# The first w_up gate columns of a decoder layer: low weights of the second unit taken by both token tiles at once, and a unit's high products set between the transposes of the second tile

## The chip, the cores and the metric

The kernel runs on one core of a Trainium2 chip. The metric is the device time of one execution in microseconds (us). The profile names the engines PE (matrix products), PEld (its weight loads), ACT, DVE, POOL and SP; SP issues most transfers.

## The reference

One decoder layer on 256 tokens of 2048 features, float32 throughout. The first half of the layer mixes tokens (two kinds of attention and an output projection), and adds the normalised result to the residual x. The change lies where the second half begins:

```python
x = x + rmsnorm(mix, post_mix_g[l])
h = rmsnorm(x, pre_ffn_g[l])
u = causal_dwconv(h @ w_up[l], conv_w[l], conv_b[l])      # w_up: 2048 x 11264
gate, val = jnp.split(u, 2, axis=-1)
y = (jax.nn.gelu(gate, approximate=True) * val) @ w_down[l]
x = x + rmsnorm(y, post_ffn_g[l])
```

## The kernel before

**Products.** Every float32 number is split in two: a high part that PE takes as it is (`whi` for weights, the first half of `hT` for the activations) and a low part, the number less its high part (`wlo`, the second half of `hT`). A product is high by high, high by low and low by high, added up in one PSUM bank. The activations stand transposed in `hT`, 16 blocks of 128 features; a block's 512 columns are the high parts of 256 tokens and then the low parts. So a block of high weights takes all 512 columns in one matmul, and a block of low weights takes 256.

**Weights.** `w_up` comes in units of 512 features by 256 columns: SP loads a unit into one of five `raw` buffers (L113), ACT makes `whi` by a copy that rounds (L168; L151 for the units named below), and DVE makes `wlo` by a subtraction that reads `raw` and `whi` (L171; L154). The `raw` buffer can be loaded again after the subtraction. Four units make the 2048 features of 256 columns.

**The first gate columns.** `first_gate` computes the first 256 gate columns, in two banks, while x and its transposes are still being made for one token tile after the other. Its four units were loaded and rounded earlier (`gate_unit`). `turn(t, n)` puts four 128x128 transposes of tile t on PE (L819), and returns two functions that fill `hT` from them: `high` on ACT (L824) and `low` on DVE (L829). Tile 1's transposes need x of tile 1, which DVE makes in four steps of 512 features (`residual`, L812). `one(t, u)` multiplies unit u for tile t: eight high matmuls over that tile's 128 high and 128 low columns (L1002), then low matmuls (L998). For units 2 and 3 (`both`) the low matmuls are left out for tile 0, and take all 256 tokens when tile 1 has come; for units 0 and 1 each tile has its own, of 128 tokens.

**After it.** `proj_T4` multiplies the first 256 value columns, then the second group of 256 gate columns, then its values, and so on. It takes four units: high products of the first and second unit (L340), their low products (L346), then low products of the third and fourth, and their high products. When a group's banks are full, each of its two blocks goes through the convolution: ACT copies half of the bank (L960), DVE adds the other half (L962), POOL multiplies by the row of norms (L963), ACT scales (L967), DVE adds two more taps (L973, L975). ACT then applies the gelu to gates (L1231), and DVE multiplies gates by values (L1249) and makes sums for the next product (L1029 to L1038, with G split by L368 and L369).

**What sets the order.** PE's order is that of the code. Around `first_gate` the same holds for ACT, DVE and POOL among their own instructions there (`order`, left right after `first_gate`). For what follows, the roundings and the convolution, a scheduler that builds the program sets each engine's order, and it may put the later roundings between the earlier work. Each engine then takes its instructions in that fixed order, and waits at the first one that isn't ready.

Of the kernel before, what the change touches and what calls it, by code (L numbers as in the profile page):

```python
# [34 lines left out]
def hybrid_layer(ctx: ExitStack, tc: tile.TileContext, x, pre_mix_g, w_in, b_forget, sinks,  # L35
# [16 lines left out]
    def bank(tag="acc"):  # L52
        return ps.tile([P, 512], F32, tag=tag, bufs=4, name="bank_" + tag)
# [9 lines left out]
    def later(n, f):  # L63
        todo.setdefault(now[0] + n, []).append(f)
# [306 lines left out]
    with tc.tile_pool(name="mixp", bufs=1) as mp:  # L371
# [442 lines left out]
        def turn(t, n):  # L814

            tb = bank("att")
            for j in range(4):
                c = n * 512 + j * P
                pe.transpose(tb[:, j * P:(j + 1) * P], x_sb[:, t, c:c + P], ident)  # L819
            kts = [(n * 4 + j, tb[:, j * P:(j + 1) * P]) for j in range(4)]  # L820

            def high():
                for kt, b in kts:
                    act.activation(hT[:, kt, t * P:(t + 1) * P], b, AF.Copy,  # L824
                                   scale=gcol[:, 16 + kt:17 + kt])

            def low():
                for kt, b in kts:
                    dve.scalar_tensor_tensor(hT[:, kt, 256 + t * P:256 + (t + 1) * P], b,  # L829
                                             gcol[:, 16 + kt:17 + kt],  # L830
                                             hT[:, kt, t * P:(t + 1) * P].bitcast(F32),
                                             op0=ALU.mult, op1=ALU.subtract)

            return high, low

        def x_squares(t):
            for n in range(4):
                act.activation(junk, x_sb[:, t, n * 512:(n + 1) * 512], AF.Square,
                               accum_out=sq2[t][:, n:n + 1])
# [63 lines left out]
    with tc.tile_pool(name="ffn", bufs=1) as fp:  # L903
# [7 lines left out]
        def ffn_tables():  # L911
            for t in range(2):
                st2 = small.tile([P, 1], F32, tag="st", name="st_x")
                dve.tensor_reduce(st2, sq2[t], axis=AX.X, op=ALU.add)
                dffn.append(diag_of(rstd_of(st2, D, f"rffn{t}")))

            def rows():
                cbk = bank("att")
                for k in range(4):
                    pe.transpose(cbk[:, k * 88:(k + 1) * 88], cst[:, k, :], ident[:88, :88])  # L920
                dve.tensor_copy(cw.rearrange("p k c -> p (k c)"), cbk[:, :352])
                dve.tensor_copy(rowf, row_of(dffn, bank("att")))

            return rows
# [54 lines left out]
        def first_gate():  # L979

            banks = [bank(), bank()]

            def one(t, u):
                ts = slice(t * P, t * P + P)

                both = u >= 2
                ls = slice(0, 256) if both else ts

                def v(x):
                    return x.rearrange("p (h t c) -> p h t c", h=2, t=2)[:, :, t, :]  # L990

                for low in (False, True)[:1 if both and t == 0 else 2]:
                    for kt in range(u * 4, u * 4 + 4):
                        hi, lo = gate[kt]
                        for m, b in enumerate(banks):
                            ms = slice(m * P, (m + 1) * P)
                            if low:
                                pe.matmul(b[:, 256 + ls.start:256 + ls.stop], lo[:, ms],  # L998
                                          hT[:, kt, ls], start=False,
                                          stop=(t == 1 and kt == KT - 1))  # L1000
                            else:
                                pe.matmul(v(b), hi[:, ms], v(hT[:, kt, :]),  # L1002
                                          start=(t == 0 and kt == 0), stop=False)

            one(0, 0)
            one(0, 1)
            one(0, 2)
            for high, low in [turn(1, u) for u in range(4)]:
                high()
                low()  # L1010
            one(0, 3)
            lows[2]()
            x_squares(0)
            x_squares(1)
            for t in range(2):
                act.dma_start(x_dram[t * P:(t + 1) * P, :], x_sb[:, t, :])
            rows = ffn_tables()
            for u in range(4):
                one(1, u)
            later(1, rows)  # L1020
            return banks
# [189 lines left out]
        for half in range(2):  # L1211
# [5 lines left out]
            for g in range(FHALF // 2):  # L1217
                c0 = (half * (FHALF // 2) + g) * 256
                alt = g % 2
                if half == 0 and g == 0:  # L1220
                    bg = first_gate()
                    order.__exit__(None, None, None)
                    bv = [bank(), bank()]
                    proj_T4(w_up, DFF + c0, bv)
                else:
                    bg = [bank("att"), bank("att")] if alt else [bank(), bank()]
                    proj_T4(w_up, c0, bg)
# [174 lines left out]
```

## Time and profile before

| what | value |
|---|---|
| median of 3 runs | 1056.29 us (1055.24 to 1056.49) |
| the profiled execution's own time | 1056.47 us |
| its span, first to last instruction | 1054.7 us |
| PE busy | 1040.4 us (99%) |
| DVE busy | 840.8 us (80%) |
| ACT busy | 660.5 us (63%) |
| POOL busy | 268.0 us (25%) |
| the first gate columns on PE | 334.49 to 349.29 us |
| the first value columns | 349.29 to 361.11 us |
| the second gate columns | from 361.11 us |

A row of the timeline has the start in us from the span's start, the time from there to the end of the last instruction merged into it, engine, line, operation, out<-in, shapes, the count, and in brackets the idle time before it with what ended it. Matmuls overlap: a row's start less the start of the row before it is what PE needs for that row. A row of another engine can overlap the next one a little in the same way.

### The profile page before, as it was taken

The page shows a single profiled execution, that of the slowest core. Times are in us where ns is not written, and L with a number is a line of the kernel's source. Part 1 is how long each engine was busy: PE and PEld are TensorE (multiplying, and loading weights), DVE is VectorE, ACT ScalarE, POOL GpSimd, SP SyncE. Part 2 cuts the span into 40 slices and gives each one's busy share as a digit, 9 for nine tenths or more (in the row PEclk, how much of TensorE's full clock was granted, in tenths as well). Part 3 has the DMA queues.
Part 4 walks back from the last instruction along what each step waited for, and adds up shares of the span by engine and source line. Part 5 has one row for each costly group of instructions (what it writes and reads, how often), then busy time and mean ns, then how long its engine had stood idle before and what let it go on. Part 6 is the DMA issues. An engine that isn't in the chain of part 4 may idle for free.

```text
span 1054.7 us, 16573 instructions
## 1 busy us (share of the span) xinstructions
PE 1040.4 (99%) x5854; PEld 907.1 (86%) x5854; DVE 840.8 (80%) x1371; ACT 660.5 (63%) x1126; POOL 268.0 (25%) x312
## 2 busy tenths in 40 slices
PE   9999999999999999999999999999999999999996
PEld 7889988888889988888888888888888888888885
DVE  5988887787467888778877799867788788779996
ACT  6767666676655865566656675646555666567771
POOL 3254325442022224232232000013223223210004
PEclk9999999999999999999999999999999999999998
DMA  8978999988872899899999796899999999969893
GB/s 282 318 240 289 296 300 304 358 251 299 318 260 68 263 250 270 222 253 258 230 244 265 262 406 192 288 237 222 284 229 243 244 233 265 232 223 384 293 410 131
DMA packets 177470, 279.98 MB, mean 265 GB/s; under 512 B 9052, under 2 KB 133244, under 8 KB 176124
## 3 DMA queue, kind: packets, MB, share of 16 engines
q1 hardware_dynamic: 162432, 249.51, 69.3%
q0 software_dynamic: 13952, 26.74, 17.8%
q10 hardware_dynamic: 1004, 2.68, 0.6%
q8 instruction: 46, 0.75, 0.3%
q14 instruction: 36, 0.29, 0.1%
HBM read 274.55 MB, written 57.69 MB: 315 GB/s over the span
## 4 chain that ended last, share of the span: by engine, by line
PE 93%; DVE 2%; DMA 2%; POOL 1%; ACT 1%; issue 1%; SPq 0%; DVEq 0%; POOLq 0%; ACTq 0%
PE bank_acc L340 16%; PE bank_att L340 14%; PE bank_acc L365 12%; PE bank_att L1044 12%; PE bank_acc L346 8%; PE bank_acc L1044 7%; PE bank_att L346 7%; PE bank_acc L309 7%; PE bank_acc L314 4%; PE bank_att L531 1%; PE bank_att L566 1%; DMA gbc_ffn<-in_post_ffn_g_dram 1%; DVE wlo L171 1%; PE bank_acc L1002 1%; POOL y_sb L1307 1%
## 5 line engine op out<-in xcount | busy, mean ns | idle before, releaser
L171 DVE TENSOR_TENSOR wlo<-raw,whi 128x1024 fp32r<-128x1024 f32 (+3 forms) x271 | 334.2, 1245 | 94.6 <-ACT whi L168 86.9
L168 ACT CAST whi<-raw 128x1024 fp32r<-128x1024 f32 (+3 forms) x270 | 273.7, 1029 | 103.5 <-issue 45.0
L963 POOL TENSOR_TENSOR room<-room,rowf 128x256 f32<-128x256 f32 x88 | 95.8, 1109 | 331.6 <-DVE room L962 329.8
L340 PE MATMUL bank_acc<-hT,whi 128*128 128x512 f32 x736 | 173.3, 390 | 0.0
L340 PEld LDWEIGHTS bank_acc<-hT,whi 128*128 128x128 f32 x736 | 136.4, 188 | 27.4
L340 PE MATMUL bank_att<-hT,whi 128*128 128x512 f32 x640 | 150.6, 390 | 0.0
L340 PEld LDWEIGHTS bank_att<-hT,whi 128*128 128x128 f32 x640 | 118.7, 188 | 23.9
L967 ACT ACTIVATE room<-room,cw 128x256 f32<-128x256 f32 x88 | 52.5, 601 | 65.3 <-POOL room L963 65.0
L346 PEld LDWEIGHTS bank_acc<-hT,wlo 128*128 128x128 f32 x736 | 89.3, 188 | 2.0
L346 PE MATMUL bank_acc<-hT,wlo 128*128 128x256 f32 x736 | 89.8, 279 | 0.0
L309 PE MATMUL bank_acc<-hT,whi 128*128 128x512 f32 x352 | 88.0, 395 | 0.0
L1044 PE MATMUL bank_att<-whi,G 128*128 128x512 f32 x258 | 87.9, 389 | 0.0
L365 PE MATMUL bank_acc<-whi,oT 128*128 128x512 f32 (+1 forms) x272 | 81.8, 379 | 0.0
L369 DVE TENSOR_TENSOR wlo<-raw,whi 128x1024 fp32r<-128x1024 f32 (+1 forms) x66 | 71.4, 1102 | 10.3 <-ACT whi L368 9.6
L346 PEld LDWEIGHTS bank_att<-hT,wlo 128*128 128x128 f32 x640 | 77.6, 188 | 1.7
L346 PE MATMUL bank_att<-hT,wlo 128*128 128x256 f32 x640 | 77.9, 279 | 0.0
L973 DVE SCALAR_TENSOR_TENSOR room<-room,cw 128x256 f32<-128x256 f32 x88 | 59.2, 676 | 22.9 <-ACT room L967 22.9
L368 ACT CAST whi<-raw 128x1024 fp32r<-128x1024 f32 (+1 forms) x66 | 61.7, 953 | 23.2 <-issue 5.7
L309 PEld LDWEIGHTS bank_acc<-hT,whi 128*128 128x128 f32 x352 | 63.3, 188 | 11.6
L365 PEld LDWEIGHTS bank_acc<-whi,oT 128*128 128x128 f32 x272 | 50.2, 188 | 9.3
L1044 PEld LDWEIGHTS bank_att<-whi,G 128*128 128x128 f32 x258 | 48.4, 188 | 10.1
L365 PE MATMUL bank_acc<-wlo,oT 128*128 128x512 f32 (+1 forms) x136 | 51.2, 377 | 0.0
(269 smaller groups left out, 1757.3 us busy)
## 6 DMA issues: line engine op xcount, KB each, us to landing
raw<-in_w_up_dram SPq DMA_DIRECT2D x176, 512.0 KB, 5.6
raw<-in_w_in_dram SPq DMA_DIRECT2D x51, 512.0 KB, 6.4
raw<-in_w_down_dram SPq DMA_DIRECT2D x45, 512.0 KB, 6.9
raw<-in_w_out_dram SPq DMA_DIRECT2D x32, 512.0 KB, 7.0
t<-in_w_down_dram POOLq DMA_DIRECT2D x28, 512.0 KB, 9.2
raw<-t SPq DMA_DIRECT2D x26, 512.0 KB, 6.6
t<-t POOLq DMA_DIRECT2D x18, 512.0 KB, 8.6
extra<-t SPq DMA_DIRECT2D x14, 512.0 KB, 6.7
```

The source lines that it names most:

```text
L168: i1 = act.copy(hi[:, cs], raw[:, cs])
L171: i2 = dve.tensor_tensor(lo[:, cs], raw[:, cs], hi[:, cs].bitcast(F32), op=ALU.subtract)
L309: pe.matmul(b, parts[u][0][:, a, m * P:(m + 1) * P], hT[:, kt, :], start=(kt == 0), stop=(kt == KT - 1))
L340: pe.matmul(b, parts[u][0][:, a, m * P:(m + 1) * P], hT[:, kt, :], start=(kt == 0), stop=(kt == KT - 1))
L346: pe.matmul(b[:, 256:512], parts[u][1][:, a, m * P:(m + 1) * P], hT[:, kt, 0:256], start=False, stop=False)
L365: pe.matmul(b, a, r[:, cols], start=(first and i == 0), stop=(last and i == 2))
L368: act.copy(hi, src)
L369: dve.tensor_tensor(lo, src, hi.bitcast(F32), op=ALU.subtract)
L963: pool.tensor_tensor(u[:, 2:258], u[:, 2:258], rowf, op=ALU.mult)
L967: act.activation(y, u[:, 2:258], AF.Identity, bias=cw[:, 3, ch:ch + 1], scale=cw[:, 2, ch:ch + 1])
L973: dve.scalar_tensor_tensor(y, u[:, 1:257], cw[:, 1, ch:ch + 1], y, op0=ALU.mult, op1=ALU.add)
L1044: pe.matmul(b[:, to] if to else b, a, r[:, cols], start=(first and i == 0), stop=(last and i == 2))
```

## The change

For unit 1 too, the low weights now wait for both token tiles: `both` begins at unit 1. And `one(0, 3)`, which then consists of eight high matmuls, stands after the second `turn` of tile 1 and not after the fourth.

```diff
-                both = u >= 2
+                both = u >= 1
...
             one(0, 0)
             one(0, 1)
             one(0, 2)
-            for high, low in [turn(1, u) for u in range(4)]:
+            turned = []
+            for u in range(4):
+                turned.append(turn(1, u))
+                if u == 1:
+                    one(0, 3)
+            for high, low in turned:
                 high()
                 low()
-            one(0, 3)
             lows[2]()
```

PE around `first_gate` before, from `one(0, 0)` on (x8 is eight matmuls in a row, 128x2x128 the high product of one tile, L819 the transposes):

```order
L1002 MATMUL bank_acc<-hT_3701,whi 128x2x128 x8
L998 MATMUL bank_acc<-hT_3701,wlo 128x128 x8
L1002 MATMUL bank_acc<-hT_3701,whi 128x2x128 x8
L998 MATMUL bank_acc<-hT_3701,wlo 128x128 x8
L1002 MATMUL bank_acc<-hT_3701,whi 128x2x128 x8
L819 MATMUL bank_att<-ident,x_sb 128x128 x16
L1002 MATMUL bank_acc<-hT_3701,whi 128x2x128 x16
L998 MATMUL bank_acc<-hT_3701,wlo 128x128 x8
L1002 MATMUL bank_acc<-hT_3701,whi 128x2x128 x8
L998 MATMUL bank_acc<-hT_3701,wlo 128x128 x8
```

And now:

```order
L1002 MATMUL bank_acc<-hT_3701,whi 128x2x128 x8
L998 MATMUL bank_acc<-hT_3701,wlo 128x128 x8
L1002 MATMUL bank_acc<-hT_3701,whi 128x2x128 x16
L819 MATMUL bank_att<-ident,x_sb 128x128 x8
L1002 MATMUL bank_acc<-hT_3701,whi 128x2x128 x8
L819 MATMUL bank_att<-ident,x_sb 128x128 x8
L1002 MATMUL bank_acc<-hT_3701,whi 128x2x128 x8
L998 MATMUL bank_acc<-hT_3701,wlo 128x128 x8
L1002 MATMUL bank_acc<-hT_3701,whi 128x2x128 x8
L998 MATMUL bank_acc<-hT_3701,wlo 128x256 x8
```

Two groups of eight low matmuls of 128 tokens are gone, one of eight of 256 tokens has come, and the transposes stand in two lots with eight high matmuls between them.

The scheduler's order behind `first_gate` is another one as well. The second gate columns have four units, called A, B, C and D here: `whi_4371`, `whi_4378`, `whi_4416`, `whi_4423` before, and `whi_4363`, `whi_4370`, `whi_4408`, `whi_4415` now (the low part has the next number; the numbers of the two programs have nothing to do with each other). ACT before, where the first gate columns go through the convolution (`bank_acc_4034` is their second bank, `bank_acc_4227` and `bank_acc_4228` those of the first values; unit A's rounding stands five rows further up):

```order
L967 ACTIVATE room_4007<-room_4002,cw_4000 128x256
L960 COPY room_4002<-bank_acc_4034 128x256
L168 CAST whi_4378<-raw_4375 128x1024
L168 CAST whi_4416<-raw_4414 128x1024
L1231 ACT_TABLE_LOAD
L1231 ACTIVATE room_4007<-room_4007 128x256
L967 ACTIVATE room_4007<-room_4002,cw_4000 128x256
L960 COPY room_4002<-bank_acc_4227 128x256
L960 COPY room_4002<-bank_acc_4228 128x256
L168 CAST whi_4423<-raw_4420 128x1024
```

And now (the first values' banks are `bank_acc_4219` and `bank_acc_4220`):

```order
L967 ACTIVATE room_4007<-room_4002,cw_4000 128x256 x2
L168 CAST whi_4363<-raw_4361 128x1024
L1235 ACT_TABLE_LOAD
L1235 ACTIVATE room_4007<-room_4007 128x256 x2
L960 COPY room_4002<-bank_acc_4219 128x256
L960 COPY room_4002<-bank_acc_4220 128x256
L168 CAST whi_4370<-raw_4367 128x1024
L967 ACTIVATE room_4007<-room_4002,cw_4000 128x256 x2
L168 CAST whi_4408<-raw_4406 128x1024
L168 CAST whi_4415<-raw_4412 128x1024
```

Before, units A, B and C were rounded ahead of the copies of the first values' banks; now A alone is, and B, C and D stand behind them. (The change adds four lines, so L1231, L1249 and L1029 are L1235, L1253 and L1033 in the changed file.)

DVE before, at the same place; unit A's low part, `wlo_4372`, stands seven rows further up:

```order
L973 SCALAR_TENSOR_TENSOR room_4007<-room_4002,cw_4000,room_4007 128x256
L962 TENSOR_TENSOR room_4002<-bank_acc_4034,room_4002 128x256
L975 SCALAR_TENSOR_TENSOR room_4007<-room_4002,cw_4000,room_4007 128x256
L171 TENSOR_TENSOR wlo_4379<-raw_4375,whi_4378 128x1024
L171 TENSOR_TENSOR wlo_4417<-raw_4414,whi_4416 128x1024
L973 SCALAR_TENSOR_TENSOR room_4007<-room_4002,cw_4000,room_4007 128x256
L962 TENSOR_TENSOR room_4002<-bank_acc_4227,room_4002 128x256
```

And now:

```order
L171 TENSOR_TENSOR wlo_4364<-raw_4361,whi_4363 128x1024
L962 TENSOR_TENSOR room_4002<-bank_acc_4219,room_4002 128x256
L962 TENSOR_TENSOR room_4002<-bank_acc_4220,room_4002 128x256
L171 TENSOR_TENSOR wlo_4371<-raw_4367,whi_4370 128x1024
L973 SCALAR_TENSOR_TENSOR room_4007<-room_4002,cw_4000,room_4007 128x256 x2
L975 SCALAR_TENSOR_TENSOR room_4007<-room_4002,cw_4000,room_4007 128x256 x2
L1253 TENSOR_TENSOR room_4007<-room_4007 128x256 x2
L1033 TENSOR_TENSOR s_4348<-room_4007 128x128
L171 TENSOR_TENSOR wlo_4409<-raw_4406,whi_4408 128x1024
L369 TENSOR_TENSOR G1_4012<-room_4007,G1_4012 128x256
L1034 TENSOR_TENSOR room_4007<-room_4007 128x128
L171 TENSOR_TENSOR wlo_4416<-raw_4412,whi_4415 128x1024
```

The low parts of C and D stand behind the whole convolution of the first values now; C's stood ahead of it before. On SP and POOL no instruction has moved, and from the values of the second group on ACT and DVE have the same order as before, but for a few neighbours that have changed places.

## The prediction

> **What bounds the kernel now.** I read the page first, its busy times and its chain, and then the waits of PE over the whole span.
>
> ```profile
> PE 1040.4 (99%) x5854; PEld 907.1 (86%) x5854; DVE 840.8 (80%) x1371; ACT 660.5 (63%) x1126; POOL 268.0 (25%) x312
> PE 93%; DVE 2%; DMA 2%; POOL 1%; ACT 1%; issue 1%; SPq 0%; DVEq 0%; POOLq 0%; ACTq 0%
> ```
>
> ```profile
> PE bank_acc L390 <- DMA x_in<-in_x_dram: 1.3, 1, 1.3
> PE bank_acc L225 <- DVE junk L220: 1.3, 1, 1.3
> PE bank_att L590 <- DVE pl L369: 1.0, 1, 1.0
> PE bank_att L578 <- DVE pl L369: 0.5, 1, 0.5
> ```
>
> PE is busy 99% of the span and is 93% of the chain. The four waits are all that the list of PE's waits has, and their lines belong to the start and to attention. So behind attention PE runs without a pause, and two things follow: PE work that goes away is gained in full, and any new wait of PE is lost in full, since no later wait could take it up. The third view is the timeline of PE at the change.
>
> ```profile
> 335.44 1.00 PE L998 MATMUL bank_acc<-hT,wlo 128*128 128x128 f32 x8
> 336.28 1.16 PE L1002 MATMUL bank_acc<-hT,whi 128*128 128x256 f32 x8
> ...
> 339.12 1.91 PE L819 MATMUL bank_att<-ident,x_sb 128*128 128x128 f32 x16
> 340.79 2.16 PE L1002 MATMUL bank_acc<-hT,whi 128*128 128x256 f32 x16
> ...
> 346.46 1.10 PE L998 MATMUL bank_acc<-hT,wlo 128*128 128x256 f32 x8
> 347.40 1.12 PE L1002 MATMUL bank_acc<-hT,whi 128*128 128x256 f32 x8
> ...
> 349.29 3.81 PE L340 MATMUL bank_acc<-hT,whi 128*128 128x512 f32 x16
> 361.11 3.80 PE L340 MATMUL bank_att<-hT,whi 128*128 128x512 f32 x16
> 364.75 3.90 PE L346 MATMUL bank_att<-hT,wlo 128*128 128x256 f32 x32
> 368.48 3.82 PE L340 MATMUL bank_att<-hT,whi 128*128 128x512 f32 x16
> ```
>
> **Part one, the low products.** Eight low matmuls of 128 tokens take 336.28 - 335.44 = 0.84, eight of 256 tokens 347.40 - 346.46 = 0.94. Two of the first go and one of the second comes: 0.94 - 2 x 0.84 = -0.74. The weights for it are there long before.
>
> **Part two, the transposes.** One low group fewer stands ahead of them, so PE comes to them 0.84 earlier, at 338.28 instead of 339.12. What they need is x of tile 1:
>
> ```profile
> 337.35 2.74 DVE L812 SCALAR_TENSOR_TENSOR x_sb<-mix_sb,rmix,x_sb 128x512 f32<-128x512 f32 x4 [0.66 <-POOL rmix L239]
> 339.76 4.25 ACT L824 ACTIVATE hT<-bank_att,gcol 128x128 fp32r<-128x128 f32 x16 [3.81 <-PE bank_att L819]
> ```
>
> The four steps of DVE end about 338.1, 338.75, 339.4 and 340.1 (2.74 in four). The first four transposes (0.42, a quarter of 340.79 - 339.12) find theirs ready at 338.28; the second four, due at 338.70, wait for 338.75 and the signal's way, some 0.17. The eight high matmuls of unit 3 then take 1.0 of PE, and the last two lots start at 340.3, behind the fourth step. So the wait is 0.17, within 0 and 0.3; without the high matmuls between, the fourth lot would have been due at 339.6 and waited half a microsecond, and that cover is what the move buys. ACT begins its 16 copies at 338.9 and not 339.76, DVE its 16 low parts at 340.15, right behind the fourth step. Tile 1's first high matmul is due at 341.15 and finds its blocks just made, as before. The first gate columns then end at 349.29 - 0.74 + 0.17 = 348.72, a gain of 0.57. The squares and the diagonal for the row of norms come earlier too: ACT has one rounding (unit A's) fewer among them.
>
> **Part three, the roundings behind it.** This is where I expect the loss. The rows of before for the second gate columns: B and C on ACT, the copies ahead of D, D; on DVE A, then B and C, then D:
>
> ```profile
> 357.74 2.00 ACT L168 CAST whi<-raw 128x1024 fp32r<-128x1024 f32 x2
> 361.86 0.63 ACT L960 COPY room<-bank_acc 128x256 f32<-128x256 f32 x2
> 362.38 1.05 ACT L168 CAST whi<-raw 128x1024 fp32r<-128x1024 f32 x1
> 351.78 1.23 DVE L171 TENSOR_TENSOR wlo<-raw,whi 128x1024 fp32r<-128x1024 f32 x1
> 358.82 2.82 DVE L171 TENSOR_TENSOR wlo<-raw,whi 128x1024 fp32r<-128x1024 f32 x2
> 363.47 1.32 DVE L171 TENSOR_TENSOR wlo<-raw,whi 128x1024 fp32r<-128x1024 f32 x1
> ```
>
> PE wanted A's and B's high parts from 361.11, their low parts from 364.75, C's low part from 364.75 + 3.73/2 = 366.61 and D's 0.93 later. C's was ready at 361.6 and D's at 364.8: 5.0 and 2.7 in hand. Now B, C and D stand behind the copies L960 of the first values' banks, which can't start until PE has ended those values, at 361.11 - 0.57 = 360.54. From there:
>
> ACT copies two banks (0.52 to the next start: 362.38 - 361.86) and rounds B from 361.06 to 362.11. PE's eight high matmuls of A end at 360.54 + 3.64/2 = 362.36, so B comes in time, by a quarter of a microsecond.
>
> Behind the copies DVE adds both banks (360.95 to 361.70), and POOL multiplies (from 361.44 and 362.03). DVE could take B's low part at 362.17. How long this takes together is the unknown, and these rows bound it:
>
> ```profile
> 356.30 0.64 POOL L963 TENSOR_TENSOR room<-room,rowf 128x256 f32<-128x256 f32 x1 [1.84 <-DVE rowf L922]
> 358.51 0.91 POOL L963 TENSOR_TENSOR room<-room,rowf 128x256 f32<-128x256 f32 x1 [1.57 <-DVE room L962]
> 374.91 2.31 POOL L963 TENSOR_TENSOR room<-room,rowf 128x256 f32<-128x256 f32 x2 [7.77 <-DVE room L962]
> 374.41 0.75 DVE L962 TENSOR_TENSOR room<-bank_att,room 128x256 f32<-128x256 f32 x2
> 375.07 1.55 DVE L171 TENSOR_TENSOR wlo<-raw,whi 128x1024 fp32r<-128x1024 f32 x1
> ```
>
> Alone, the product L963 takes 0.64. At 358.51 it began 0.31 ahead of a subtraction, took 0.91, and the pair of subtractions took 2.82: with 1.2 for the second, 1.6 for the first. At 374.91 the subtraction began inside the first product and ahead of the second, which was held up: the two took 2.31, so the second 1.7. Whichever is first is nearly undisturbed. Here POOL's second product, at 362.03, is ahead of B's subtraction by 0.14: POOL ends at 362.7, and DVE is free again at 363.75. I take this, the nearest row being 358.51.
>
> The Trainium skill has a rule for it, on the page "SBUF — State Buffer", section "SBUF: two separate sides": DVE, when it reads two inputs in SBUF, and GpSimd share one pair of ports as an exclusive lock, and the one that starts second is blocked for the other's whole instruction. The trace agrees (0.64 alone, 1.7 behind a subtraction). By the rule the order of the two decides, and the sum is 1.5 or that of the first rival below; if they merely shared the speed, either order would cost alike, and that rival would go.
>
> Then ACT scales (L967, one after each product, to 363.3) and rounds C from 363.24 to 364.29. But DVE has the convolution of the values ahead of C's low part: two L973, two L975, two L1249, one L1029. Its length stands in these rows:
>
> ```profile
> 366.05 0.48 DVE L973 SCALAR_TENSOR_TENSOR room<-room,cw 128x256 f32<-128x256 f32 x1 [0.39 <-ACT room L967]
> ...
> 368.12 1.22 DVE L171 TENSOR_TENSOR wlo<-raw,whi 128x1024 fp32r<-128x1024 f32 x1
> 369.26 0.42 DVE L369 TENSOR_TENSOR G<-room,G 128x256 fp32r<-128x256 f32 x1
> ...
> 369.80 1.22 DVE L171 TENSOR_TENSOR wlo<-raw,whi 128x1024 fp32r<-128x1024 f32 x1
> ```
>
> 368.12 - 366.05 = 2.07 with one L973, and 0.4 more for the other: from 363.75 to 366.2. C's low part is made until 367.4 (1.22). PE, without a pause so far, wants it at 360.54 + 3.64 + 3.73/2 = 366.05, and waits till 367.45: **1.4**. Eight low matmuls of C later (0.93) PE wants D's, at 368.38. DVE first splits G and takes a difference (369.80 - 369.26 = 0.54) and then makes it, 367.3 + 0.54 + 1.22 = 369.05: a second wait, **0.7**. D's high part and those of the next units are there by then. After that DVE and ACT have PE's whole high products of C and D (3.65) to catch up in, and the order is the old one.
>
> The `raw` buffers come free later too: A's at 360.2, where it was 353.0 (351.78 and 1.2), C's at 367.4, where it was 361.6. The loads that SP issues into them are for the next values, and start 7 us later behind A, 3 to 6 behind the others:
>
> ```profile
> raw<-in_w_up_dram SPq DMA_DIRECT2D x176, 512.0 KB, 5.6
> 378.49 1.05 ACT L168 CAST whi<-raw 128x1024 fp32r<-128x1024 f32 x1 [4.70 <-DMA raw<-in_w_up_dram]
> ```
>
> Before, ACT waited 4.7 for such a load and PE did not notice. With 5.6 from issue to landing the load behind A lands at 366, and ACT wants it at 366.5; the one behind C lands at 373, and PE wants that unit's low part near 380. I cost this at nothing; at 10 us a load the cover would be just used up.
>
> **The sum**: -0.74 + 0.17 + 1.4 + 0.7 = +1.5. The profiled execution took 1056.47, its span 1054.7; the sum is a difference inside the span, so it would give 1058.0 for that execution. The median is 0.18 lower: **1057.8 us**. A measurement of this kernel tells about 0.2%, 2.1 us, from no change, so I forecast no change that can be told, on the slow side.
>
> **The rivals.**
>
> *The subtraction goes first.* If B's subtraction starts ahead of POOL's second product (0.14 decides), that one ends 0.6 behind it, as at 374.91: at 364.3 rather than 362.7. ACT scales till 364.95, rounds C till 365.9, DVE's convolution ends at 367.05, C's low part is there at 368.3 and D's at 370: waits of 2.3 and 0.7, and the sum is +2.45, **1058.75**, slower by 0.23%. For it speaks that the pair at 374.91 went this way; against it, that there the subtraction didn't have to wait for ACT, and here it does.
>
> *No wait.* If ACT and DVE keep ahead of PE in spite of their order (the copies of the banks could start earlier than I think, and C's low part come by 366), only the first two parts are left: -0.57, **1055.7**. For it speaks the 5.0 that C had in hand, and that ACT is busy 63% only; against it, that both engines take their rows in order, and that 1.4 has to be found in a chain whose links all have a row.
>
> *The loads are late.* If the loads behind C and D land 10 us after C's release and then wait in turn, the second group's values wait 1 to 2 us more: 1059.5. ACT's 4.7 at 378 speak for it, PE's lack of a wait there against.
>
> **How the numbers follow.** My case 0.62, the subtraction first 0.2, no wait or a small one 0.12, late loads 0.06. My case alone has 1057.1 to 1058.5, from the wait of part two (0 to 0.3) and 0.3 either way in each later wait. The range reaches from a small wait to the subtraction first: 1056.4 to 1059.1. Slower by over 0.2% (above 1058.4) are the second case, most of the last, and little of mine: 0.26. Faster by over 0.2% would need a gain of 2.1, where 0.74 is all that PE loses in work: 0.02. Within: 0.72.
>
> **What would show it.** In the profile of the changed kernel: the first gate columns on PE end about 348.7, with one small wait at the second lot of transposes (L819 behind DVE's L812). The wait list of PE has a new entry, L346 behind DVE's L171, twice, 1.4 and 0.7, near 367 and 369. POOL's product at 362 takes 0.64 to 0.9, and the subtraction beside it 1.6; 1.2 to 1.55 there and 1.7 at POOL is the first rival. No entry of L346 at all is the second, and an entry of ACT's L168 behind a DMA with PE waiting after it is the third. The forecast is wrong if PE's time from 334.5 to the end of the second gate columns doesn't grow by 1 to 2 us, or if PE waits somewhere behind them.

## The result, and the profile after

The changed kernel takes 1058.70 us (median of 9 runs, 1057.87 to 1059.57), the kernel before in the same set 1055.96 (9 runs, 1055.24 to 1056.97): a ratio of 1.0027, with a 95% interval of 1.0018 to 1.0036. It is slower by 2.7 us. The forecast was 1057.8 us, within 1056.4 to 1059.1, and "no change that can be told". The time lies in the range; the verdict that I held likeliest did not come: 0.27% is over the 0.2% that I had set, and the interval leaves out 1.

Busy time and chain of the changed kernel's page:

```profile
PE 1040.8 (98%) x5846; PEld 905.4 (86%) x5846; DVE 843.3 (80%) x1371; ACT 659.0 (62%) x1126; POOL 269.0 (25%) x312
...
PE 91%; DVE 3%; DMA 2%; ACT 1%; POOL 1%; issue 1%; SPq 0%; DVEq 0%; POOLq 0%; ACTq 0%
```

PE has eight instructions fewer, and its share of the span and of the chain falls from 99% and 93% to 98% and 91%: PE stands still somewhere it didn't before. The list of PE's waits names the place; this line is new in it:

```profile
PE bank_att L346 <- DVE wlo L171: 2.0, 3, 1.3
```

The timeline of PE (start, time, instruction, and in brackets the idle time ahead of it with what ended it) shows where, and what the first gate columns have become:

```profile
333.29 1.12 PE L1002 MATMUL bank_acc<-hT,whi 128*128 128x256 f32 x8
...
337.05 1.24 PE L819 MATMUL bank_att<-ident,x_sb 128*128 128x128 f32 x8
338.04 1.20 PE L1002 MATMUL bank_acc<-hT,whi 128*128 128x256 f32 x8
339.07 1.04 PE L819 MATMUL bank_att<-ident,x_sb 128*128 128x128 f32 x8
340.06 1.34 PE L1002 MATMUL bank_acc<-hT,whi 128*128 128x256 f32 x8
...
347.81 3.81 PE L340 MATMUL bank_acc<-hT,whi 128*128 128x512 f32 x16
...
363.28 2.03 PE L346 MATMUL bank_att<-hT,wlo 128*128 128x256 f32 x16
366.62 1.21 PE L346 MATMUL bank_att<-hT,wlo 128*128 128x256 f32 x8 [1.31 <-DVE wlo L171]
368.29 1.21 PE L346 MATMUL bank_att<-hT,wlo 128*128 128x256 f32 x8 [0.47 <-DVE wlo L171]
369.35 7.43 PE L340 MATMUL bank_att<-hT,whi 128*128 128x512 f32 x32
376.61 1.09 PE L346 MATMUL bank_att<-hT,wlo 128*128 128x256 f32 x8
377.98 3.48 PE L346 MATMUL bank_att<-hT,wlo 128*128 128x256 f32 x24 [0.27 <-DVE wlo L171]
```

Two profiled executions don't start alike: this one reaches the first gate columns at 333.29, that of before at 334.49, and nothing is changed ahead of them. So I compare lags: when the same instruction of PE starts here, less when it starts in the profile of before. The lag is -1.20 at the start of the first gate columns and -1.48 at their end (347.81 against 349.29): they gain 0.28. It is +0.87 where the high products of C and D begin (369.35 against 368.48): 2.35 lost at the waits for C's and D's low parts. When the second group's values are done it is +1.78: another 0.91 lost. From there to the last matmul it grows by 0.35 more, which belongs to this execution: the two later profiles of the same kernel (below) have 0.13 and 0.00 there. Forecast were 0.57, 2.1 and 0.

Split by the rows: the sixteen low matmuls from 363.28 take 3.73/2 = 1.87, so C's were due at 365.15 and came at 366.62, **1.47** late; eight later (0.93) D's were due at 367.55 and came at 368.29, **0.74** late; the high products came 0.13 behind their time. I had 1.4 and 0.7. (The brackets count from the end of the row before, which overlaps the next; so they show less, 1.31 and 0.47.)

On DVE and POOL of the changed kernel:

```profile
361.28 1.69 DVE L171 TENSOR_TENSOR wlo<-raw,whi 128x1024 fp32r<-128x1024 f32 x1 [0.47 <-ACT whi L168]
362.90 0.87 DVE L973 SCALAR_TENSOR_TENSOR room<-room,cw 128x256 f32<-128x256 f32 x2
...
365.36 1.21 DVE L171 TENSOR_TENSOR wlo<-raw,whi 128x1024 fp32r<-128x1024 f32 x1
...
367.03 1.21 DVE L171 TENSOR_TENSOR wlo<-raw,whi 128x1024 fp32r<-128x1024 f32 x1
```

```profile
360.56 1.34 POOL L963 TENSOR_TENSOR room<-room,rowf 128x256 f32<-128x256 f32 x2 [4.41 <-DVE room L962]
361.84 0.96 POOL L94 DMA_DIRECT2D t<-in_w_down_dram  x1
362.51 1.14 POOL L94 DMA_DIRECT2D t<-t  x1
```

This is the chain of the prediction, link by link, 0.9 earlier on this clock (0.28 of gain in place of 0.57, and the start 1.2 earlier): B's subtraction begins 0.12 behind POOL's second product (361.16; I had 0.14) and is the one held up (1.69, where it takes 1.21 alone; the two products take 1.34 together), then the convolution, then C's low part at 365.36 and D's at 367.03.

What the forecast lacked is on ACT, in the second group's values. Their first and second unit are rounded by 366.6; the third comes 6.6 us later:

```profile
362.44 2.93 ACT L168 CAST whi<-raw 128x1024 fp32r<-128x1024 f32 x3
...
365.58 1.04 ACT L168 CAST whi<-raw 128x1024 fp32r<-128x1024 f32 x1
373.17 1.05 ACT L168 CAST whi<-raw 128x1024 fp32r<-128x1024 f32 x1 [6.55 <-PE bank_att L340]
```

The row puts this wait down to PE's high products. But the unit's load goes into B's `raw` buffer, which B's subtraction gives free at 362.97, and one of the transfers issued then is

```profile
raw<-in_w_up_dram SPq DMA_DIRECT2D x1, 512.0 KB, 10.1
```

issued at 363.00, landed at 373.07, a tenth of a microsecond ahead of the rounding. In the kernel before, the load behind B took 5.1. POOL's two accumulating DMAs stand right behind its products for the values. In the kernel before:

```profile
362.89 2.49 POOL L963 TENSOR_TENSOR room<-room,rowf 128x256 f32<-128x256 f32 x2 [3.47 <-DVE room L962]
365.32 0.96 POOL L94 DMA_DIRECT2D t<-in_w_down_dram  x1
```

There they went out at 365.32 and 366.00, long behind this load (360.53); here at 361.84 and 362.51, ahead of it. From 363 to 367, right behind its issue, the list of packets by queue has one line, POOL's queue (packets, MB, share of the time of 16 DMA engines):

```profile
q0 software_dynamic: 212, 0.43, 92.0%
```

Not one packet of SP's load moved in these four microseconds. Which of the two explanations holds, PE's products or the load, is the fourth experiment's question.

How the late rounding would reach PE stands on DVE:

```profile
374.56 0.43 DVE L369 TENSOR_TENSOR G<-room,G 128x256 fp32r<-128x256 f32 x1 [6.12 <-ACT G L368]
...
375.10 1.22 DVE L171 TENSOR_TENSOR wlo<-raw,whi 128x1024 fp32r<-128x1024 f32 x1
```

ACT's rounding of G (L368) stands behind the late one, DVE's split of G (L369) waits 6.12 us for it, and the low parts of the second values' first two units stand behind that split. So PE waits for low parts whose own weights had been rounded by 366.6.

### The profile page after: what moved, and what is told of

Same layout as the page of the kernel before. It is cut to its first block, busy times and chain, and to the rows that moved or that the text cites. A ratio compares the mean times of both kernels' runs of the same rounds, so it can differ in the third digit from the quotient of the medians.

```text
span 1057.6 us, 16554 instructions
## 1 busy us (share of the span) xinstructions
PE 1040.8 (98%) x5846; PEld 905.4 (86%) x5846; DVE 843.3 (80%) x1371; ACT 659.0 (62%) x1126; POOL 269.0 (25%) x312
## 4 chain that ended last, share of the span: by engine, by line
PE 91%; DVE 3%; DMA 2%; ACT 1%; POOL 1%; issue 1%; SPq 0%; DVEq 0%; POOLq 0%; ACTq 0%
PE bank_acc L340 15%; PE bank_att L340 13%; PE bank_acc L365 12%; PE bank_att L1048 12%; PE bank_acc L346 8%; PE bank_acc L1048 7%; PE bank_acc L309 7%; PE bank_att L346 7%; PE bank_acc L314 4%; DVE wlo L171 1%; PE bank_att L531 1%; PE bank_att L566 1%; DMA gbc_ffn<-in_post_ffn_g_dram 1%; PE bank_acc L1002 1%; DMA x_in<-in_x_dram 1%
## 5 line engine op out<-in xcount | busy, mean ns | idle before, releaser
L168 ACT CAST whi<-raw 128x1024 fp32r<-128x1024 f32 (+3 forms) x270 | 273.9, 1029 | 106.3 <-issue 39.2
L346 PEld LDWEIGHTS bank_acc<-hT,wlo 128*128 128x128 f32 x736 | 89.3, 188 | 2.0
L346 PE MATMUL bank_acc<-hT,wlo 128*128 128x256 f32 x736 | 89.9, 279 | 0.0
L346 PEld LDWEIGHTS bank_att<-hT,wlo 128*128 128x128 f32 x640 | 78.0, 188 | 4.6 <-DVE wlo L171 2.6
L346 PE MATMUL bank_att<-hT,wlo 128*128 128x256 f32 x640 | 79.2, 280 | 2.0 <-DVE wlo L171 2.0
L369 DVE TENSOR_TENSOR wlo<-raw,whi 128x1024 fp32r<-128x1024 f32 (+1 forms) x66 | 71.5, 1106 | 9.0 <-ACT whi L368 8.3
L368 ACT CAST whi<-raw 128x1024 fp32r<-128x1024 f32 (+1 forms) x66 | 61.6, 952 | 22.1 <-issue 4.9
```

What stands on the lines that cost most here:

```text
L168: i1 = act.copy(hi[:, cs], raw[:, cs])
L346: pe.matmul(b[:, 256:512], parts[u][1][:, a, m * P:(m + 1) * P], hT[:, kt, 0:256], start=False, stop=False)
L368: act.copy(hi, src)
L369: dve.tensor_tensor(lo, src, hi.bitcast(F32), op=ALU.subtract)
```

## The experiments

For all of them the table gives what PE gained (-) or lost (+) against the profile of before, as differences of lags: in the first gate columns, behind them up to the high products of C and D, and from there to the end of the second group's values.

| kernel | first gate columns | C and D | second values | sum | ratio to before |
|---|---|---|---|---|---|
| changed kernel | -0.28 | +2.35 | +0.91 | +2.98 | 1.0027 |
| 1: move only | 0.00 | 0.00 | 0.00 | 0.00 | 1.0000 |
| 2: low products only | -0.17 | +2.35 | +0.69 | +2.87 | 1.0031 |
| 3: order kept | -0.63 | 0.00 | 0.00 | -0.63 | 0.9994 |
| 4: POOL's DMAs later | -0.62 | +3.90 (both) | | +3.28 | 1.0018 |
| 5: order kept, loads by SP | -0.64 | 0.00 | 0.00 | -0.64 | 0.9995 |
| 6: order kept, again | -0.48 | 0.00 | 0.00 | -0.48 | 0.9994 |
| 7: changed kernel, again | -0.63 | +2.33 | +0.53 | +2.23 | 1.0026 |
| 8: as 4 | -0.47 | +2.35 | +0.02 | +1.90 | one run |
| 9: as 4 | -0.63 | +2.35 | -0.02 | +1.70 | one run |
| 10: changed kernel, a third time | -0.58 | +2.34 | +0.39 | +2.15 | one run |

**Experiments 1 and 2: one part alone.** The first leaves the low products as before and only moves the last unit's high products; the second is the other half. Against the changed kernel:

```diff
 experiment 1
-                both = u >= 1
+                both = u >= 2
 experiment 2
-                if u == 1:
-                    one(0, 3)
             for high, low in turned:
                 high()
                 low()
+            one(0, 3)
```

> Only the move: the high matmuls of the last unit stand between the second and the third lot of transposes, and the low weights of the second unit meet the two token tiles apart, as before. The instructions of ACT, DVE, POOL and SP stand in the order of the kernel before, row by row. Theory 'order' (the loss is the new order of the roundings, not the new place of anything on PE): no wait of PE at L346 near 367, the same work on PE, the transposes at the same time as before; first gate columns end within 0.2 us of where they did, ratio 0.999 to 1.001. Rival 'place' (the split run of transposes and matmuls is what costs): the gate columns end 0.5 us or more later, or a wait of over 0.5 us shows behind them, and the ratio is 1.001 or more.

> Only the low products: the second unit's low weights meet both tiles at once, the last unit's high matmuls stand behind all transposes as before. The rows of ACT, DVE, POOL and SP are those of the changed kernel. Theory 'order': the waits of PE at L346 are there as in the changed kernel (1.3 and 0.5 near 367 and 368, 0.9 together behind 376), less the 0.1 to 0.5 that PE comes later to them, since the last two lots of transposes now wait for x; 2.4 to 3.2 us more than before, ratio 1.0023 to 1.0030. Rival 'place': without the split run the 0.74 us of PE work that goes are a gain, ratio 0.9993.

Measured: 1056.39 us for the move (12 runs) and 1059.40 for the low products (7 runs), before 1056.24; ratios 1.0000 (0.9992 to 1.0009) and 1.0031 (1.0021 to 1.0041). PE of the first experiment:

```profile
332.21 1.12 PE L1002 MATMUL bank_acc<-hT,whi 128*128 128x256 f32 x8
...
347.01 3.81 PE L340 MATMUL bank_acc<-hT,whi 128*128 128x512 f32 x16
...
362.47 3.90 PE L346 MATMUL bank_att<-hT,wlo 128*128 128x256 f32 x32
```

and of the second:

```profile
337.50 2.56 PE L819 MATMUL bank_att<-ident,x_sb 128*128 128x128 f32 x16
...
348.38 3.81 PE L340 MATMUL bank_acc<-hT,whi 128*128 128x512 f32 x16
...
367.21 1.20 PE L346 MATMUL bank_att<-hT,wlo 128*128 128x256 f32 x8 [1.32 <-DVE wlo L171]
368.88 1.20 PE L346 MATMUL bank_att<-hT,wlo 128*128 128x256 f32 x8 [0.48 <-DVE wlo L171]
```

The move by itself does nothing: 14.80 us from the start to the end of the first gate columns, as before, and all 32 low matmuls of the second gate columns in one run. The low products by themselves bring the whole loss, and they bring the new order of the roundings with them. 'Place' (the split run of transposes is what costs) is out. The sixteen transposes in one run take 2.32 to the next matmul, where they took 1.67: 0.65 of waiting for x, about the 0.17 and the half microsecond that the prediction gave for the case without cover. With the gain of 0.17 that makes 0.82 of work gone from PE, where I had 0.74. So the move is worth something only once the low products have gone.

**Experiment 3: the order kept.** Everything on PE is as in the changed kernel. Unit A's load and rounding are written ahead of the convolution of the first gate columns instead of behind it:

```diff
-    def proj_T4(w, c0, banks):
+    def proj_T4(w, c0, banks, parts=None):
...
-        parts = {}
+        parts = {} if parts is None else parts
...
-            for u in us:
+            for u in [u for u in us if u not in parts]:
...
-                    proj_T4(w_up, DFF + c0, bv)
+                    proj_T4(w_up, DFF + c0, bv); soon = {u: w_split(w_load(w_rows(w_up, u * 4, 4, 256, 256), 4, 256), still=True) for u in range(1)}
...
-                    proj_T4(w_up, c0, bg)
+                    proj_T4(w_up, c0, bg, soon if half == 0 and g == 1 else None)
```

This one rounding tips the scheduler back (why the low products had tipped it was not looked into). ACT's rows, changed kernel (-) against this one (+). The first row with + is unit A's rounding, which stood where the L168 with - stands; the last row with + is B's and C's, which in the changed kernel stand further down, behind the copies L960 of the first values' banks:

```
-L960 COPY room<-bank_acc 128x256
+L168 CAST whi<-raw 128x1024
 L838 ACTIVATE junk,sqm_3704<-x_sb 128x512
 L960 COPY room<-bank_acc 128x256
 L838 ACTIVATE junk,sqm_3704<-x_sb 128x512
 L1020 DMA x_dram<-x_sb 128x2048 x2
-L967 ACTIVATE room<-room,cw 128x256 x2
-L168 CAST whi<-raw 128x1024
+L967 ACTIVATE room<-room,cw 128x256
+L960 COPY room<-bank_acc 128x256
+L168 CAST whi<-raw 128x1024 x2
```

> The whole change on PE, but the rounding of the first unit of the second gate columns (unit A) is written one place earlier in the program, ahead of the convolution of the first gate columns. The scheduler then orders ACT and DVE through the second gate columns as in the kernel before: A ahead of the first bank copies, B and C ahead of the copies of the first values' banks. Theory 'order': no wait of PE at L346 by these units; what is left is the gain of the first gate columns, 0.3 us as the changed kernel showed it up to 0.57 as I had it; 1055.4 to 1055.7 where before is 1056.0, ratio 0.9994 to 0.9997. Rival 'pace' (PE's coming 0.3 us earlier is enough to make it wait, or the loads collide whatever the order): waits of 1 us or more at L346 remain, ratio 1.001 or more.

Measured: 1055.28 us (11 runs), ratio 0.9994 (0.9986 to 1.0003). ACT and PE:

```profile
356.44 2.00 ACT L168 CAST whi<-raw 128x1024 fp32r<-128x1024 f32 x2
```

```profile
333.83 1.12 PE L1002 MATMUL bank_acc<-hT,whi 128*128 128x256 f32 x8
...
348.00 3.81 PE L340 MATMUL bank_acc<-hT,whi 128*128 128x512 f32 x16
...
363.46 3.90 PE L346 MATMUL bank_att<-hT,wlo 128*128 128x256 f32 x32
```

B and C are rounded together at 356.44, ahead of the copies; PE has its 32 low matmuls in one run, and no wait behind the first gate columns. POOL's first DMA goes out at 364.04, on this clock where it did before (365.32 there). The lag is -0.66 at their start and -1.29 from their end to the last matmul. With the same work on PE, one order costs 3 us and the other gains 0.6: 'pace' (PE's coming earlier is enough to make it wait) is out, and the loss of the changed kernel is the order's, the late load included.

**Experiment 4: POOL's two DMAs later.** The changed kernel, with the accumulating DMAs of that place held until a few loads later:

```diff
-            while steps and owed[span] >= steps[0][0]:
+            while steps and owed[span] >= steps[0][0] and not 112 <= loads[0] < 119:
```

> The changed kernel, but POOL issues its two accumulating DMAs (issued there at 361.84 and 362.51) only behind the next gate columns' products, some 19 us later. Nothing else moves. Theory 'load' (the 0.94 us that PE loses behind 376 come from the load that SP issues at 363.00 and that landed 10.1 us later, since POOL's two DMAs were ahead of it): the load lands in 5 to 6 us, ACT's rounding that began at 373.2 begins near 368.5, and the waits behind 376 go; those of 1.3 and 0.5 stay; 0.9 us less than the changed kernel, ratio to before 1.0016 to 1.0020. Rival 'buffer' (that rounding waited for PE to be done with its high buffer, as the trace's row has it: PE bank_att L340): it begins near 373 again, the ratio stays at 1.0025 to 1.0029.

Measured: 1057.75 us (12 runs, 1055.91 to 1059.58), ratio 1.0018 (1.0010 to 1.0026). PE's wait list has L346 with 1.8 in two waits; there is none behind 376. ACT rounds the unit at once, in one row with the one ahead of it, where there had been one cast and then 6.55 of idle time:

```profile
365.46 1.99 ACT L168 CAST whi<-raw 128x1024 fp32r<-128x1024 f32 x2
```

'Load' holds, 'buffer' is out. But this profile lost 3.90 between the first gate columns and 372, not the 2.35 of the others. The rows of the granted clock (stretch, its length, PE's busy time and matmuls, clock, DMA share, GB/s):

```profile
364.00:366.00 2.00, 1.20 (x11) 1.00 0.79 259
366.00:368.00 2.00, 1.20 (x8) 1.00 0.14 36
368.00:370.00 2.00, 1.82 (x8) 0.56 0.84 252
370.00:372.00 2.00, 2.00 (x8) 0.59 0.90 268
372.00:374.00 2.00, 2.00 (x11) 1.00 0.74 225
```

Right behind the two waits PE ran at little over half its clock for some 3 us, which cost 3.90 - 2.35 = 1.55 us. The profiles of the changed kernel and of the second experiment, with the same waits, do not show this. Whether it belongs to the kernel or to the execution is asked below.

**Experiments 5 and 6: the version with the order kept, with one change and once more.** In the changed kernel's profile the first gate columns gained 0.28 only. Ahead of tile 1's copies (L824) ACT issues four small loads:

```profile
335.61 2.42 ACTq L906 DMA_DIRECT2D cst<-in_conv_w_dram  x3
338.05 0.38 ACTq L907 DMA_DIRECT2D cst<-in_conv_b_dram  x1
338.48 4.24 ACT L824 ACTIVATE hT<-bank_att,gcol 128x128 fp32r<-128x128 f32 x16 [3.72 <-PE bank_att L819]
```

so ACT was free only at 338.43 and began the copies 1.43 behind the start of the transposes (338.48 against 337.05). The fifth experiment gives these loads to SP:

```diff
-            act.dma_start(cst[:, k, :], conv_w[k].rearrange("(a p) -> a p", p=P))
-        act.dma_start(cst[:, 3, :], conv_b[0].rearrange("(a p) -> a p", p=P))
+            sp.dma_start(cst[:, k, :], conv_w[k].rearrange("(a p) -> a p", p=P))
+        sp.dma_start(cst[:, 3, :], conv_b[0].rearrange("(a p) -> a p", p=P))
```

> The whole change with the order of the roundings kept (as in the third experiment), and the four loads of the convolution's weights and biases issued by SP, which had no load to issue between 332 and 345, in place of ACT. Theory 'issue time' (in the changed kernel's profile the first gate columns gained only 0.29 us, since ACT was held by issuing these loads, L906 for 2.42 us, until 338.43, and its first copy L824 came 0.4 to 0.6 us late; where L906 took 1.27 to 1.80 us the gain was 0.6): ACT's copies L824 begin within 0.3 us of the end of the first lot of transposes, PE's first high matmul of tile 1 has no wait, the gain of the first gate columns is 0.57 to 0.65; ratio 0.9992 to 0.9996. Rival 'x' (the transposes' and the copies' time is set by DVE's additions for tile 1 alone): the copies begin as in the third experiment and the gain is as there, 0.63; the ratio is the same.

> The kernel of the third experiment once more, for a narrower interval: the whole change with the order of the roundings as before. Theory 'order': ratio 0.9994, 0.6 us less than before, in this set too; rival: the 0.9994 of the first set was chance, and the ratio is 1.000 or above.

Measured: 1055.84 us (11 runs), ratio 0.9995 (0.9987 to 1.0004), and 1055.85 (11 runs), 0.9994 (0.9985 to 1.0003), before 1056.32. In the sixth, L906 took long again:

```profile
334.99 2.23 ACTq L906 DMA_DIRECT2D cst<-in_conv_w_dram  x3
```

Over all profiles with both parts of the change, the first gate columns gained 0.58 to 0.63 where L906 took 1.27 to 2.12 us (experiments 3, 4, 7, 9, 10), 0.47 and 0.48 where it took 2.23 (8 and 6), and 0.28 where it took 2.42. With the loads on SP they gained 0.64, and ACT began the copies 0.64 behind the start of the transposes:

```profile
340.36 1.23 PE L819 MATMUL bank_att<-ident,x_sb 128*128 128x128 f32 x8
```

```profile
341.00 4.23 ACT L824 ACTIVATE hT<-bank_att,gcol 128x128 fp32r<-128x128 f32 x16 [2.94 <-PE bank_att L819]
```

So 'issue time' holds for those executions in which the issue is slow, and 'x' for the others: it is a hold-up of up to 0.35 that comes and goes, and on SP it is gone. That is too little for the ratio.

The version with the order kept beats the changed kernel clearly (0.9994 against 1.0026 to 1.0027). That it beats the kernel before is shown by the profiles, 0.48 to 0.64 us within the span, and by three medians on the same side; each interval by itself reaches just past 1.

**Experiments 7 to 10: the changed kernel and the fourth experiment's, again.** The kernels are the same, word for word.

> The changed kernel once more, unaltered. In the fourth experiment's profile PE's granted clock was 0.50 to 0.67 for 3 us right behind the two waits at L346, at a cost of 1.5 us, in the first profile of the changed kernel and in the second experiment's, with the same waits, it was 1.0. If this is a matter of chance in each execution, this profile shows either; the wait list shows L346 behind DVE's L171 with 1.8 to 2.0 in any case, and the ratio to before is 1.002 to 1.0036. If the delay of POOL's two DMAs brought the low clock, it stays 1.0 here. For the gain of the first gate columns: 0.6 where L906 takes 1.3 to 1.8 us, 0.3 where it takes 2.4.

> The kernel of the fourth experiment (POOL's two DMAs later) once more, one profile. If the low clock behind its waits at L346 is a matter of each execution (where the two waits fall against whatever the clock's control looks at), this profile may show 1.0, and then PE's loss from 365 to 372 is 2.3 us and not 3.8, and the execution takes about 1057.5. If the kernel itself brings it, the clock is 0.5 to 0.67 again. In either case ACT's rounding behind the load that SP issues at 363 begins by 367, and there is no loss behind 376.

> The same again, for the same question: clock of 1.0 (the execution's chance) or 0.5 to 0.67 (the kernel's own).

> The changed kernel a third time, one profile. Chance: a low clock of 0.5 to 0.67 may show behind its waits too, and then the execution takes over 1060; without it, waits of 1.3 and 0.5 at L346, 0.5 to 0.9 lost behind 376, and an execution near 1058.5.

Measured: the changed kernel again 1058.63 us (10 runs), ratio 1.0026 (1.0016 to 1.0035); the three single runs 1057.87, 1057.13 and 1059.04, beside 1055.28 for before. All four have the two waits at L346, 1.8 together, and a granted clock of 1.00 in every stretch behind them. So the low clock of the fourth experiment is a matter of the execution, once in the seven profiles that have these waits, and the price of the waits without it is 2.33 to 2.35 in each of six. In the ninth, the load that took 10.1 in the changed kernel and the roundings behind it are

```profile
raw<-in_w_up_dram SPq DMA_DIRECT2D x1, 512.0 KB, 3.4
```

```profile
365.04 1.99 ACT L168 CAST whi<-raw 128x1024 fp32r<-128x1024 f32 x2
```

and the second values lose nothing (0.02 and -0.02). In the tenth, the changed kernel's own, the trace itself names the load where the first profile had named PE:

```profile
373.08 1.05 ACT L168 CAST whi<-raw 128x1024 fp32r<-128x1024 f32 x1 [6.03 <-DMA raw<-in_w_up_dram]
```

There the second values lose 0.39, in the seventh 0.53, in the second 0.69: the late load is a part of the change's price, of 0.4 to 0.9.

## Why the prediction was right, and where it fell short

**Part one** (-0.74) **and part two** (+0.17, gain 0.57): right. The undisturbed profiles gain 0.58 to 0.63; by the rows it is 0.82 of work less 0.20 of waiting. The wait at the second lot of transposes is there (eight of them take 338.04 - 337.05 = 0.99; in the first experiment, where x was ready, 337.64 - 336.85 = 0.79), and so is the cover of the high matmuls, as the second experiment measured without it. Not foreseen was that ACT's own issue of loads could hold the copies; I had set the copies' start by the transposes alone.

**Part three, the waits** (1.4 and 0.7): right in place, order and size: 1.47 and 0.74, and 0.13 behind them that I didn't have. That the order of the two engines' rows, and not anything on PE, decides was the heart of the forecast, and the third experiment shows it by keeping the order.

**The first rival** (the subtraction first) didn't occur: POOL's two products took 1.34 together, the subtraction 1.69. The rule of the Trainium skill quoted in the prediction (page "SBUF — State Buffer", section "SBUF: two separate sides"), that the one of DVE and GpSimd that starts second is blocked, fits these rows roughly: blocked until POOL's end at 361.90, the subtraction would end at 363.11, and it ended at 362.97. **No wait** didn't occur either.

**The late loads: here the forecast fell short.** The step that failed is "I cost this at nothing". I went through the loads behind A and C with the 5.6 us that a load took, and put the time of 10 us into a rival with a chance of 0.06. The load that came late was the one behind B, and it came late for a reason I had not followed: POOL's DMAs moved in time, though no instruction on POOL moved in order. In the kernel before, its second product stood behind D's subtraction, and the two products took 2.49; here they began 0.85 earlier and took 1.34. So the two accumulating DMAs behind them went out 2.0 earlier (361.84 against 365.32, on clocks that lie 1.48 apart there), while B's subtraction and so this load came 4.0 later (363.00 against 360.53). The rival's mechanism thus occurred together with my own case, at half its price: 0.4 to 0.9 in place of 1 to 2.

**The sum.** Forecast: -0.57 + 1.4 + 0.7 = +1.5. Measured in the three profiles of the changed kernel: -0.28 to -0.63, +2.33 to +2.35, +0.39 to +0.91, together +2.15 to +2.98, in line with medians 2.7 and 2.3 above before. Of the 1.45 that the forecast lacks in the first profile, 0.91 is the load, 0.29 the first gate columns and 0.25 the waits. The verdict turned on this: +1.5 is within 0.2% (2.1 us), and the load's share is what carries the change beyond it: without it the fourth experiment has 1.0018.

The prediction's own sign of being wrong, that PE waits somewhere behind the second gate columns, did show (377.98). And that the time is in the range is in part luck: 1058.70 is above what my case alone allowed (1057.1 to 1058.5), and the range reached so far only for the first rival, which didn't occur.

## What to carry to other kernels

A gain on the engine that bounds the kernel can move the point at which a scheduler picks an instruction on the others; before the gain is counted, compare the order of every engine, and pin or rewrite the order that had slack (here one rounding, written one place earlier, turned +3 us into -0.6). When an instruction moves on one queue, follow the transfers that other queues issue right behind it: not only whether a load still has time, but which transfers are now ahead of it. And let a wait's releaser be checked against landings when the time fits another cause to a tenth of a microsecond.

## What the runs showed of the hardware

- Behind 2.2 us of standing still within 3.1 (1.47 and 0.74, between 365.0 and 368.2 in the fourth experiment) PE's granted clock fell to 0.56 to 0.59 in rows of 2 us (0.50 in the lowest of 1 us) for some 3 us in one of seven profiles, at a cost of 1.55 us; in the other six, with the same two waits, it stayed at 1.00. The Trainium skill, page "TensorE: Matmul & The Clock Gate", section "Part 1: The HAM clock gate (the "warmup" mystery)", has the clock fall to half after an idle window of about 3.4 us, and says that this window runs freely and isn't reset when a kernel starts. No gap here was that long; that one execution in seven is hit fits a free-running window, the length of the gap doesn't. What sets it off was not tried.
- The time that ACT needs to issue the same three small loads varied from 1.27 to 2.42 us between executions. What it depends on stays open.
- The same load of 512 KB took 5.1 us in the kernel before, 3.4 in the ninth experiment with nothing of POOL's ahead of it, and 9.5 to 10.1 in the four profiles in which POOL's two accumulating DMAs were issued just ahead of it (0.5 and 1.2 us in the first). In those profiles the load hardly moved at first: from 364 to 368 the second and the seventh experiment have 223 and 222 packets of POOL's queue and 1 and none of SP's. In the ninth SP's queue moved 528 packets, 0.52 MB, from 362.9 to 366.
